# A third gate/up column pair by seven products, and first weight sums of the output products by accumulating transfers

## The chip, the core and the metric

The kernel runs on one core of a Trainium2 chip. TensorE (PE in the profile) multiplies, ScalarE (ACT) and VectorE (DVE) prepare weights and finish results, GpSimd (POOL) takes a few roots and issues accumulating DMAs, and SyncE (SP) issues the other DMAs. The metric is the device time of one execution in microseconds (us); of several runs the median counts.

## The reference

Two layers of a decoder trunk work on 256 tokens with 1024 channels. In each layer a retention mixer and a state-space (SSD) mixer feed a gated sum, and a SwiGLU feed-forward network (FFN) with 2816 hidden columns follows. What the change touches is in these lines:

```python
o_ret = yr @ ret_out                      # 2048 -> 1024
o_ssd = ys @ ssd_out                      # 2048 -> 1024
merged = sigmoid(gate_ret) * o_ret + sigmoid(gate_ssd) * o_ssd
h = h + merged @ w_o
...
gu = rmsnorm(h, norm_ffn_w) @ w_gate_up   # 1024 -> 2 * 2816
gate, up = split(gu, [2816])
h = h + (silu(gate) * up) @ w_down        # 2816 -> 1024
```

## The kernel before

**Precision.** Every float32 operand is split in two float32r parts, a high one and the rest. A product is three matmuls: high by high, high by low, low by high (`mm3`, L542). For a weight piece of 128x1024 the split is one ACT instruction (`wh`, L506) and one DVE subtraction (`wl`, L527). Seven pairs of `wh` and `wl` buffers are there (`HB`, L200): a piece can be split at most seven pieces ahead of TensorE.

**Three ways to compute a pair of FFN columns.** The hidden columns are cut into five pairs of 512 gate and 512 up columns, and a half pair (number 5, `NPAIR`). `FFN` (L1142) lists how each is computed, in the order of the jobs.
- `plain`: eight weight pieces, 96 matmuls of 512 columns, and the result of each token tile is transposed (`up_post`, L1939) since the down product needs it with channels on partitions.
- `fm` (`fm_job`, L970): four jobs, also eight pieces. The weights stand still and the tokens move, so the result comes out transposed already. A job has two blocks, each with eight matmuls of 512 columns and eight of 256.
- `seven` (`sevens`, L359, and `wino_job`, L911): the 2x2 block product of two token tiles by two halves of the 1024 channels by gate and up columns, with seven block products in place of eight: 84 matmuls of 512 columns. It needs sums of weight blocks: t1 = 11 + 12, t2 = t1 + 22, t3 = 12 + 22, t4 = t2 + 21. Each of the seven (11, t1, t2, 22, t3, 21, t4) is two pieces, so 14 pieces are split. The tokens' sums are made once per layer (`seven_sums`, L675), on DVE and ACT, and the results of the blocks are put together on DVE. Its result is transposed as in `plain`.

`GF` (L32) names the pairs whose weights are laid out for `fm`.

**Sums of weights.** A sum is either a DVE addition (L230 in the profile) or, where `added` names it, a DMA that POOL issues and that adds weights from DRAM to the buffer in place (L416). Such a DMA can only be issued when both splits of what stood in the buffer have been made, and the next split waits until it has landed.

**Output products.** `out_wino` (L1057) does a part of each of `ret_out`, `ssd_out` and `w_down` by seven products and the other rows of the weights plainly, one 128x1024 piece at a time, with four blocks (two token tiles t0, t1 by two column halves) of three matmuls each. An order such as `AMID` (L294, for `w_down`) says how the seven products and the plain pieces (`"*"`) follow each other. The plain pieces that the order doesn't name come last, and block by block: all of them for t0 and the first half of the columns, then t0 and the second half, then t1 twice. So the residual sum, the norm and the transposition for t0 can begin while TensorE still works for t1. `w_down` has 14 plain pieces; `AMID` names nine of them, and five are left for the end.

**Order of the work.** The kernel plans itself while it is built: every step is put on its engine's instruction list when a model of the engines, with priorities by job number, says that it is due (`Flow`). On the chip each engine then works through its list strictly in that order, and an instruction that waits holds up all behind it. Raw weight pieces land in four `raw` buffers; the seven products also use two buffers called `raws` (block 11) and two called `cc` (block 12), or `dec` in the retention product.

Of the kernel before, what the change touches and what calls it, by code (L numbers as in the profile page):

```python
# [27 lines left out]
NPAIR = FF // 512  # L28
C_Q, C_K, C_V, C_G, C_Z, C_X, C_DT, C_GR, C_GS = 0, 1024, 2048, 4096, 6144, 8192, 11264, 11296, 12320
NB = 24  # L30

GF = (1, 3, NPAIR)  # L32


DW = 1
# [157 lines left out]
def trunk_kernel(  # L193
# [66 lines left out]
    ccS, new_cc = pooled(tp, (P, D), F32, "cc", 2)  # L260
# [30 lines left out]
    ALONE = ("11", "t1", "t2", "22", "t3", "21", "t4")  # L291


    AMID = ("*", "*", "*", "*", "11", "*", "t1", "*", "t2", "22", "*", "t3", "*", "21", "*", "t4")  # L294

    SMID = ("*", "*", "11", "*", "t1", "*", "t2", "22", "*", "t3", "21", "t4")

# [759 lines left out]
    def out_wino(op, nk, at, tag, order, post, add, ops):  # L1057
# [74 lines left out]
        for t in range(NT):  # L1132
# [7 lines left out]


    FFN = [[("plain", 0)],  # L1142
           [("fm", 1)],
           [("seven", (2,), ("t3", "t4"))],
           [("fm", 3)],
           [("seven", (4,), ("t3", "t4"))],
           [("fm", NPAIR)]]
    DIRECT = ()
    DOWN_APART = ()

# [14 lines left out]
    def add_layer_jobs(l):  # L1165
        def srcs_of(kind, *at):
            if kind == "gr":
                return tm_srcs(w_gr[l, at[0]])
            if kind in FM:
                return fm_srcs(w_fm[l, FM[kind] + at[0] + (at[0] + at[1] if len(at) > 1 else 0)])  # L1170
            if kind in ("ret", "ssd", "wo"):
                return out_srcs({"ret": ret_out, "ssd": ssd_out, "wo": w_o}[kind][l])
            return tm_srcs(w_tm[l, TM[kind] + at[0]], kper=1 if l == 0 and (kind, *at) == ("v", 0) else 2)

        def adds_of(kind, *at, order=MIXED):
            if kind == "seven":
                c = TM[at[0]] + at[1]
                return [sevens(w_tm[l, c], w_tm[l, c + 1], added=at[2], order=order, slots=None)]
            return [plain((srcs_of(kind, *at), APARTS.get((kind, *at), ())))]

        for m in MIXERS[l]:
            if m == ("ret",):
                group(sevens(w_rw[l, 0], w_rw[l, 1], added=("t3", "t4"), order=RMID, first=RET_FIRST),
                      plain((out_srcs(ret_out[l])[8:], RET_APART)))
            elif m == ("ssd",):
                group(sevens(w_sw[l, 0], w_sw[l, 1], added=("t3", "t4"), order=SMID, slots=(ccS, new_cc)),
                      plain((out_srcs(ssd_out[l])[8:], ())))
            elif isinstance(m, tuple):
                for add in adds_of(*m, order=ALONE):
                    group(add)  # L1190
            else:
                group(*(chain(*(a for j in stream for a in adds_of(*j))) for stream in m))
        for members in FFN:
            adds = []
            for kind, *at in members:
                if kind == "seven":
                    adds.append(chain(*(sevens(w_gate_up[l, 0, c], w_gate_up[l, 1, c], added=at[1], order=ALONE if len(members) == 1 else ASIDE,
                                               slots=(ccS, new_cc)) for c in at[0])))
                elif kind == "fm":
                    adds.append(plain(*((srcs, APART) for c in at for srcs in gf_srcs(l, c))))  # L1200
                else:
                    adds.append(plain(*((srcs, APART) for c in at for srcs in gate_up_srcs(l, c))))
            group(*adds)
        lone = [s for k, s in enumerate(out_srcs(w_down[l])) if k // 4 not in (DW, DW + 1)]
        group(sevens(w_dw[l, 0], w_dw[l, 1], added=("t3", "t4"), order=AMID, slots=(ccS, new_cc)),
              plain((lone, DOWN_APART)))

    def params(l, done):
# [1011 lines left out]
```

## Time and profile before

| | |
|---|---|
| Median of 3 runs | 1253.82 us (1253.73 to 1256.33) |
| The profiled execution's own time | 1254.82 us |
| Its span, first to last instruction | 1253.0 us |
| Instructions in it | 17610 |
| Moved by DMA | 266.27 MB, mean 213 GB/s |
| FFN of the first layer on TensorE | about 450 to 629 us |
| FFN of the second layer | about 1069 us to the end |

A page of the profile gives busy times, the chain of work that ended last, and groups of instructions by line. The trace behind it can be asked for single instructions in order of time ("the timeline"), for busy times in stretches ("the windows"), and for the instructions of one line with their shortest, median and longest duration. Matmuls overlap in their pipeline: a row shows 0.39 us for a matmul of 512 columns, while the next one starts after about 0.23 us. So costs on TensorE are read from start to start. The same holds on DVE, where instructions overlap a little.

### The profile page before, as it was taken

How to read it: one execution, taken by the hardware profiler on the slowest of the kernel's cores; microseconds unless marked ns; L12 is line 12 of the kernel's file. 1: busy time of each engine (PE TensorE's matmuls, PEld its weight loads, DVE VectorE, ACT ScalarE, POOL GpSimd, SP SyncE). 2: the span in 40 equal slices, each digit the busy share in tenths (PEclk: the TensorE clock that was granted, in tenths of full speed). 3: DMA queues.
4: the chain of work that ended last, by engine and by line, in shares of the span. 5: the costliest groups of instructions: out<-in, count | busy, mean ns of one | idle time of the engine just before them, and what ended most of it. 6: DMA issues, size and time to landing. Idle time of an engine off the chain costs nothing.

```text
span 1253.0 us, 17610 instructions
## 1 busy us (share of the span) xinstructions
PE 1241.8 (99%) x6286; PEld 1051.5 (84%) x6286; DVE 1108.0 (88%) x1516; ACT 885.2 (71%) x1307; POOL 67.2 (5%) x92
## 2 busy tenths in 40 slices
PE   9999999999999999999999999999999999999997
PEld 7889888888888888888888898888888888888886
DVE  6997888789999978999888888888899998899995
ACT  6866778877776566776586676878877674776753
POOL 0000000000002001001000000000010110010000
PEclk9999999999999999999999999999999999999999
DMA  8758565456768657877777475555667676678872
GB/s 289 253 145 285 182 187 166 152 190 185 258 232 225 233 187 226 296 210 215 256 249 235 112 259 167 188 168 165 217 179 241 240 231 218 216 212 252 290 205 85
DMA packets 76343, 266.27 MB, mean 213 GB/s; under 512 B 8768, under 2 KB 9024, under 8 KB 76256
## 3 DMA queue, kind: packets, MB, share of 16 engines
q1 hardware_dynamic: 68416, 237.25, 55.8%
q0 software_dynamic: 7552, 27.38, 11.7%
q8 instruction: 49, 0.80, 0.3%
q10 hardware_dynamic: 288, 0.52, 0.1%
q14 instruction: 38, 0.31, 0.1%
HBM read 262.96 MB, written 2.16 MB: 212 GB/s over the span
## 4 chain that ended last, share of the span: by engine, by line
PE 91%; ACT 4%; DVE 2%; issue 1%; DMA 1%; SPq 0%; POOL 0%; POOLq 0%; ACTq 0%; DVEq 0%
PE acc L543 19%; PE acc L545 19%; PE acc L544 19%; PE acc L988 14%; PE acc L989 8%; PE tr L640 2%; PE yps L1699 2%; PE acc L991 2%; ACT wh L506 1%; DVE wl L527 1%; ACT seg L1667 1%; PE acc L1421 1%; PE tr L1592 1%; DMA raw<-in_w_gr_dram 1%; DMA raw<-in_w_tm_dram 1%
## 5 line engine op out<-in xcount | busy, mean ns | idle before, releaser
L527 DVE TENSOR_TENSOR wl<-raw,wh 128x1024 fp32r<-128x1024 f32 (+2 forms) x388 | 458.4, 1195 | 52.7 <-ACT wh L506 48.7
L506 ACT ACTIVATE wh<-raw 128x1024 fp32r<-128x1024 f32 (+2 forms) x388 | 397.2, 1035 | 148.2 <-PE acc L545 37.1
L988 PE MATMUL acc<-xT,wh 128*128 128x512 f32 x840 | 303.8, 399 | 0.3 <-DVE cc L230 0.3
L989 PE MATMUL acc<-xT,wl 128*128 128x256 f32 x960 | 252.2, 281 | 0.0
L543 PE MATMUL acc<-wh,xT 128*128 128x512 f32 (+1 forms) x568 | 220.1, 387 | 0.0
L545 PE MATMUL acc<-wh,xT 128*128 128x512 f32 (+1 forms) x568 | 216.1, 380 | 0.0
L544 PE MATMUL acc<-wl,xT 128*128 128x512 f32 (+1 forms) x568 | 216.1, 380 | 0.0
L989 PEld LDWEIGHTS acc<-xT,wl 128*128 128x128 f32 x960 | 181.2, 189 | 10.1
L988 PEld LDWEIGHTS acc<-xT,wh 128*128 128x128 f32 x840 | 158.0, 188 | 32.9 <-PE acc L991 0.6
L544 PEld LDWEIGHTS acc<-wl,xT 128*128 128x128 f32 x568 | 106.7, 188 | 20.2 <-issue 1.0
L543 PEld LDWEIGHTS acc<-wh,xT 128*128 128x128 f32 x568 | 106.7, 188 | 19.5 <-issue 1.4
L545 PEld LDWEIGHTS acc<-wh,xT 128*128 128x128 f32 x568 | 106.6, 188 | 19.5
L506 ACT ACTIVATE wh<-raws 128x1024 fp32r<-128x1024 f32 x80 | 83.5, 1057 | 32.0 <-DVE raws L230 12.9
L527 DVE TENSOR_TENSOR wl<-raws,wh 128x1024 fp32r<-128x1024 f32 x80 | 96.3, 1220 | 7.9 <-ACT wh L506 7.5
L543 PE MATMUL acc<-wh,A 128*128 128x512 f32 x224 | 89.9, 402 | 0.3
L545 PE MATMUL acc<-wh,A 128*128 128x512 f32 x224 | 87.5, 390 | 0.0
L544 PE MATMUL acc<-wl,A 128*128 128x512 f32 x224 | 87.3, 390 | 0.0
L233 DVE SCALAR_TENSOR_TENSOR cc<-cc,cv 128x255 f32<-128x255 f32 (+1 forms) x144 | 67.1, 478 | 2.5 <-ACT cc L223 1.6
L223 ACT ACT_TABLE_LOAD x43 | 55.2, 1283 | 6.1 <-DVE cc L233 5.5
L543 PE MATMUL acc<-wh,C 128*128 128x512 f32 (+1 forms) x152 | 59.3, 390 | 0.0
L544 PE MATMUL acc<-wl,C 128*128 128x512 f32 (+1 forms) x152 | 58.4, 384 | 0.9 <-DVE wl L527 0.9
L545 PE MATMUL acc<-wh,C 128*128 128x512 f32 (+1 forms) x152 | 58.2, 383 | 0.0
(197 smaller groups left out, 1999.7 us busy)
## 6 DMA issues: line engine op xcount, KB each, us to landing
raw<-in_w_tm_dram SPq DMA_DIRECT2D x104, 512.0 KB, 4.2
raw<-in_w_fm_dram SPq DMA_DIRECT2D x80, 512.0 KB, 4.2
raw<-in_w_gf_dram SPq DMA_DIRECT2D x40, 512.0 KB, 4.6
raw<-in_w_gate_up_dram SPq DMA_DIRECT2D x32, 512.0 KB, 6.3
raw<-in_w_down_dram SPq DMA_DIRECT2D x28, 512.0 KB, 4.7
raw<-in_w_gr_dram SPq DMA_DIRECT2D x24, 352.0 KB, 3.9
seg<-acs SPq DMA_DIRECT2D x16, 512.0 KB, 5.1
raw<-in_ret_out_dram SPq DMA_DIRECT2D x16, 512.0 KB, 4.2
```

The costliest lines, as they stand in the source:

```text
L223: return Op("act", cost, lambda: nc.scalar.activation(out=out, in_=in_, func=func, **kw), pr, TABLES.get(func))
L233: return Op("dve", 1.04 * n + 130, lambda: nc.vector.scalar_tensor_tensor(out=out, in0=in0, scalar=scalar, in1=in1, op0=op0, op1=op1), pr)
L506: nc.scalar.activation(out=wh[:, :m], in_=raw[:, :m], func=AF.Copy)
L527: nc.vector.tensor_tensor(out=wl[:, :m], in0=raw[:, :m], in1=wh[:, :m].bitcast(F32), op=ALU.subtract)
L543: nc.tensor.matmul(ps, lhsT=lh, rhs=rh, start=first, stop=False, **kw)
L544: nc.tensor.matmul(ps, lhsT=lh, rhs=rl, start=False, stop=False, **kw)
L545: nc.tensor.matmul(ps, lhsT=ll, rhs=rh, start=False, stop=last, **kw)
L640: nc.tensor.transpose(out=ps[:, j * P : (j + 1) * P], in_=src[:, j * P : (j + 1) * P], identity=ident)
L988: nc.tensor.matmul(a, lhsT=wh[:, k % 4, fsl], rhs=x[:, k % 4, :, :], start=k == 0, stop=False)
L989: nc.tensor.matmul(a[:, :SEQ], lhsT=wl[:, k % 4, fsl], rhs=xh[:, k % 4, :], start=False, stop=False)
L991: nc.tensor.matmul(a, lhsT=wh[:, k % 4, fsl], rhs=x[:, k % 4, :, :], start=False, stop=True)
L1699: nc.tensor.matmul(ps[:, i * HD : (i + 1) * HD], lhsT=sg[:, i, :], rhs=xdt[:, i * HD : (i + 1) * HD], start=True, stop=True)
```

## The change

Three things are edited.
- `FFN` and `GF`: before, the pairs ran as plain 0, fm 1, seven 2, fm 3, seven 4, fm half pair 5. Now they run as plain 0, seven 1, fm 2, seven 3, fm half pair 5, seven 4. So per layer one `fm` pair becomes a `seven` pair, and a seven pair now follows the plain pair at once, one follows the half pair, and one stands directly ahead of the down product.
- `added=("t1", "t3", "t4")` for the sevens of `ret_out`, `ssd_out` and `w_down`: the first sum, t1, is made by an accumulating DMA and no longer on DVE. As block 12 is then needed in a buffer for t3 alone, its load is placed later (`need`, L375). The sevens of the FFN pairs keep t1 on DVE.
- `AMID`: eight plain pieces ahead of the first seven-product block instead of four, eleven named instead of nine. Three are left for the end instead of five.

```diff
-GF = (1, 3, NPAIR)
+GF = (2, NPAIR)
...
-    AMID = ("*", "*", "*", "*", "11", "*", "t1", "*", "t2", "22", "*", "t3", "*", "21", "*", "t4")
+    AMID = ('*', '*', '*', '*', '*', '*', '*', '*', '11', '*', 't1', '*', 't2', '22', '*', 't3', '21', 't4')
...
     FFN = [[("plain", 0)],
-           [("fm", 1)],
-           [("seven", (2,), ("t3", "t4"))],
-           [("fm", 3)],
-           [("seven", (4,), ("t3", "t4"))],
-           [("fm", NPAIR)]]
+           [("seven", (1,), ("t3", "t4"))],
+           [("fm", 2)],
+           [("seven", (3,), ("t3", "t4"))],
+           [("fm", NPAIR)],
+           [("seven", (4,), ("t3", "t4"))]]
...
-                group(sevens(w_rw[l, 0], w_rw[l, 1], added=("t3", "t4"), order=RMID, first=RET_FIRST),
+                group(sevens(w_rw[l, 0], w_rw[l, 1], added=("t1", "t3", "t4"), order=RMID, first=RET_FIRST),
...
-                group(sevens(w_sw[l, 0], w_sw[l, 1], added=("t3", "t4"), order=SMID, slots=(ccS, new_cc)),
+                group(sevens(w_sw[l, 0], w_sw[l, 1], added=("t1", "t3", "t4"), order=SMID, slots=(ccS, new_cc)),
...
-        group(sevens(w_dw[l, 0], w_dw[l, 1], added=("t3", "t4"), order=AMID, slots=(ccS, new_cc)),
+        group(sevens(w_dw[l, 0], w_dw[l, 1], added=("t1", "t3", "t4"), order=AMID, slots=(ccS, new_cc)),
```

What that does to the engines' lists shows at three places.

The first is on DVE in the first layer, right behind the plain pair, while the tokens' sums (`plain`, `D`) are made; `wl` is the low part of a weight piece, `raws` and `raw` the blocks 11 and 22 or pieces of an fm pair, `sil` and `A` the plain pair's result. Before, these twelve rows stood there:

```order
L230 TENSOR_TENSOR plain_4449<-plain_4449,plain_4537 128x512
L527 TENSOR_TENSOR wl_4610<-raw_4524,wh_4594 128x1024
L230 TENSOR_TENSOR D_4609<-plain_4449,D_4608 128x4x128
L230 TENSOR_TENSOR plain_4531<-plain_4425,plain_4531 128x512
L527 TENSOR_TENSOR wl_4628<-raw_4576,wh_4617 128x1024
L527 TENSOR_TENSOR wl_4639<-raw_4584,wh_4630 128x1024
L230 TENSOR_TENSOR D_4609<-plain_4531,D_4608 128x4x128
L527 TENSOR_TENSOR wl_4661<-raw_4603,wh_4646 128x1024
L230 TENSOR_TENSOR sil_4502<-acc_4503,sil_4502 128x512
L230 TENSOR_TENSOR sil_4586<-acc_4587,sil_4586 128x512
L527 TENSOR_TENSOR wl_4686<-raw_4622,wh_4670 128x1024
L230 TENSOR_TENSOR sil_4694<-acc_4667,sil_4694 128x256
```

Now twelve rows of the same stretch, up to the `wl` of t2's second piece (`wl_4720`), are these:

```order
L230 TENSOR_TENSOR raws_4480<-raws_4480,cc_4494 128x1024
L230 TENSOR_TENSOR D_4613<-plain_4539,D_4612 128x4x128
L230 TENSOR_TENSOR raws_4475<-raws_4475,raw_4499 128x1024
L230 TENSOR_TENSOR sil_4510<-acc_4511,sil_4510 128x512
L230 TENSOR_TENSOR sil_4592<-acc_4593,sil_4592 128x512
L527 TENSOR_TENSOR wl_4668<-raws_4480,wh_4645 128x1024
L527 TENSOR_TENSOR wl_4673<-raws_4475,wh_4657 128x1024
L230 TENSOR_TENSOR raws_4480<-raws_4480,raw_4507 128x1024
L230 TENSOR_TENSOR A_4663<-tr_4676,A_4662 128x4x128
L230 TENSOR_TENSOR A_4663<-tr_4682,A_4662 128x4x128
L527 TENSOR_TENSOR wl_4710<-raw_4507,wh_4699 128x1024
L527 TENSOR_TENSOR wl_4720<-raws_4480,wh_4708 128x1024
```

The additions of weight blocks (`raws<-raws`) now stand among the tokens' sums, and t2's second low part stands behind both of its sums. The second layer has the same rows.

The second place is DVE's list between the end of the first layer's down product and the second layer. `O` is the residual, two buffers for t0 and t1; `ms` belongs to the norm, `sil` is the normed input, `xT` its transposed low part, `wl` are weights of the second layer. Before:

```order
L230 TENSOR_TENSOR O_3863<-O_3863,acc_5624 128x512
L238 TENSOR_SCALAR ms_6037<-ss_6036,ms_6018 128x1
L233 SCALAR_TENSOR_TENSOR sil_6048<-O_3863,rstd_6043,wb_5620 128x512
L233 SCALAR_TENSOR_TENSOR sil_6049<-O_3863,rstd_6043,wb_5620 128x512
L230 TENSOR_TENSOR O_3866<-O_3866,acc_5629 128x512
L230 TENSOR_TENSOR xT_6055<-tr_6057,xT_6055 128x4x128
```

Now:

```order
L230 TENSOR_TENSOR O_3860<-O_3860,acc_5575 128x512
L527 TENSOR_TENSOR wl_6030<-raw_5977,wh_6017 128x1024
L238 TENSOR_SCALAR ms_6016<-ss_6015 128x1
L238 TENSOR_SCALAR ms_6029<-ss_6028,ms_6016 128x1
L230 TENSOR_TENSOR O_3864<-O_3864,acc_5583 128x512
L527 TENSOR_TENSOR wl_6060<-raw_5989,wh_6037 128x1024
L233 SCALAR_TENSOR_TENSOR sil_6055<-O_3860,rstd_6046,wb_5570 128x512
L233 SCALAR_TENSOR_TENSOR sil_6056<-O_3860,rstd_6046,wb_5570 128x512
L230 TENSOR_TENSOR O_3864<-O_3864,acc_5590 128x512
L238 TENSOR_SCALAR ms_6059<-ss_6058 128x1
L527 TENSOR_TENSOR wl_6094<-raw_5995,wh_6049 128x1024
L230 TENSOR_TENSOR xT_6074<-tr_6077,xT_6074 128x4x128
```

Three weight splits and both residual sums of t1 now stand between t0's last residual sum and the first `xT`. On TensorE the transposition of t0 (`tr_6057` before, `tr_6077` now) stood ahead of the last block of the down product before; now it stands behind it.

The third place is POOL's list in the SSD output product of the first layer; `rz` is a root of the norm there, `raws` holds block 11 and then t1, t2, t4, and `cc` holds block 12 and then t3. The rows with + are new, the one with - goes:

```order
 L668 DMA wb<-in_ssd_norm_w_dram 128x1024
+L416 DMA raws<-in_w_sw_dram 128x1024
+L243 TENSOR_TENSOR rz<-ms,mhalf 128x1 x2
+L416 DMA raws<-in_w_sw_dram 128x1024
 L243 TENSOR_TENSOR rz<-ms,mhalf 128x1 x2
 L416 DMA cc<-in_w_sw_dram 128x1024 x2
-L243 TENSOR_TENSOR rz<-ms,mhalf 128x1 x2
 L668 DMA wb<-in_norm_ffn_w_dram 128x1024
 L416 DMA raws<-in_w_sw_dram 128x1024 x2
```

The two new DMAs make t1. The pairs of roots that stood around the `cc` transfers now stand behind one or both of them.

## The prediction

> **What bounds the kernel now.** I read the page's busy times first, then the chain that ended last, then the windows of the first layer's FFN, where most of the change lies.
>
> ```profile
> PE 1241.8 (99%) x6286; PEld 1051.5 (84%) x6286; DVE 1108.0 (88%) x1516; ACT 885.2 (71%) x1307; POOL 67.2 (5%) x92
> ...
> PE 91%; ACT 4%; DVE 2%; issue 1%; DMA 1%; SPq 0%; POOL 0%; POOLq 0%; ACTq 0%; DVEq 0%
> ```
>
> TensorE is busy for 99% of the span and carries 91% of the chain. DVE is next with 88%. So time is won where TensorE gets less to do, as long as DVE, which prepares its weights, doesn't fall behind. The windows below go from one job's first matmul to the next one's: plain 0, fm 1, seven 2, fm 3, seven 4, the half fm, the down product.
>
> ```profile
> core 0: us, PE busy (x) PEld busy (x) DVE busy (x) ACT busy (x) POOL busy (x), PEclk, DMA share, GB/s
> 450.45:473.32 22.87, 22.87 (x106) 19.03 (x105) 20.71 (x26) 17.28 (x24) 0.55 (x1) 1.00 0.66 220
> 473.32:496.76 23.44, 23.44 (x138) 20.46 (x137) 20.01 (x25) 13.61 (x20) 2.61 (x3) 1.00 0.80 238
> 496.76:515.80 19.04, 19.04 (x85) 15.77 (x84) 19.03 (x21) 15.73 (x19) 0.88 (x1) 1.00 0.78 215
> 515.80:539.20 23.40, 23.40 (x137) 20.48 (x136) 21.19 (x26) 15.35 (x23) 2.60 (x3) 1.00 0.88 274
> 539.20:558.24 19.04, 19.04 (x85) 15.77 (x84) 19.02 (x21) 15.73 (x19) 0.87 (x1) 1.00 0.79 215
> 558.24:570.37 12.13, 12.13 (x74) 10.68 (x72) 9.29 (x12) 8.72 (x13) 0.00 (x0) 1.00 0.96 372
> 570.37:628.80 58.43, 58.27 (x261) 48.02 (x260) 51.45 (x62) 34.04 (x44) 4.58 (x6) 1.00 0.71 211
> ```
>
> Three things stand there. TensorE has no gap in the pairs, at full clock (1.00). While it does a seven pair, DVE is full (19.03 of 19.04 us). DVE's total over the seven windows is 160.70 us (the sum of their third column), TensorE's 178.35.
>
> ```profile
> L543 PEld LDWEIGHTS acc<-wh,xT 128*128 128x128 f32 x568 | 106.7, 188 | 19.5 <-issue 1.4
> 496.75 0.40 PE L543 MATMUL acc<-wh,xT 128*128 128x512 f32 x1
> 513.08 0.39 PE L543 MATMUL acc<-wh,xT 128*128 128x512 f32 x1
> ```
>
> Between the last two rows lie 72 matmuls of seven 2, so one starts 0.227 us after the other, and each has a weight load of 0.188 us, 83% of that. The Trainium skill, "Perfetto Trace Analysis", section "Identifying the Most-Contended Engine", says that matmul busy time tells little about how full TensorE is and that weight-load busy time is the better measure. By it the page's 84% would leave 16% to win without less work; the 83% inside a row without gaps says that 84% is full here, and the sum below is unchanged.
>
> **TensorE's gain.** Per layer an fm pair goes and a seven pair comes.
>
> ```profile
> 473.32 0.39 PE L988 MATMUL acc<-xT,wh 128*128 128x512 f32 x1
> ...
> 475.90 0.40 PE L991 MATMUL acc<-xT,wh 128*128 128x512 f32 x1
> 476.13 1.03 PE L640 MATMUL tr<-cst,sil 128*128 128x128 f32 x8
> ...
> 477.25 0.28 PE L989 MATMUL acc<-xT,wl 128*128 128x256 f32 x1
> ```
>
> The first block of fm 1 runs from 473.32 to 0.23 behind 475.90: 2.81 us, and a pair has eight. The eight transpositions that plain and seven results need, set into the next job, cost 1.35 us from 475.90 to 477.25 less the two matmuls of 0.23 around them: 0.88. The windows of fm 1 and fm 3 less this are 22.56 and 22.52, so an fm pair takes 22.54. A seven pair takes 19.04 (its window). So a pair saves 22.54 - 19.04 - 0.88 = 2.62 us, and the two layers **5.24 us**.
>
> **DVE's price.**
>
> ```profile
> 481.40 1.23 DVE L527 TENSOR_TENSOR wl<-raws,wh 128x1024 fp32r<-128x1024 f32 x1 [0.20 <-ACT wh L506]
> 482.66 1.22 DVE L230 TENSOR_TENSOR raws<-raws,cc 128x1024 f32<-128x1024 f32 x1
> ...
> 507.01 2.35 DVE L527 TENSOR_TENSOR wl<-raws,wh 128x1024 fp32r<-128x1024 f32 x2
> ...
> 608.37 4.63 DVE L527 TENSOR_TENSOR wl<-raw,wh 128x1024 fp32r<-128x1024 f32 x4
> ```
>
> Four splits in a row take 4.63, so a further one costs (4.63 - 1.22)/3 = 1.14 us; an addition takes the same 1.22 by itself. A seven pair has 14 splits and 4 additions of 1.14 (20.5) and eight combinations of about 0.6: 25.3 us. An fm pair has eight splits (9.1) and its combinations, some 5.1: 14.2. DVE gets 11.1 us more per layer, and the down product's t1 by DMA takes two additions (2.3) away. That makes 169.5 us in the FFN against 175.7 on TensorE: 96%. It fits on the whole; the question is where it doesn't in places.
>
> Where a seven pair follows a full fm pair, as seven 3 does, nothing differs from before: the first low part of seven 2 is made at 481.40, more than 14 us ahead of 496.75, and its last pair ends at 509.36, some 5 us ahead of its use near 514.7. Seven 4 now follows a half fm. DVE's work for both is 7.1 + 25.3 = 32.4 us, TensorE's 12.13 + 19.04 = 31.17; with those 5 us at the start some 3.9 us remain at the end. I cost it at nothing; its cover is that lead.
>
> **Seven 1 behind the plain pair** has no such start.
>
> ```profile
> 460.01 0.69 DVE L230 TENSOR_TENSOR plain<-plain 128x512 f32<-128x512 f32 x1 [0.67 <-ACT plain L223]
> 461.40 0.69 DVE L230 TENSOR_TENSOR D<-plain,D 128x512 fp32r<-128x512 f32 x1 [0.70 <-ACT D L223]
> ```
>
> From this `plain` row to the second low part of t2 (`wl_4720`) the new list has 24 rows: eight splits and four additions at 1.14, and twelve of about 0.61: 21.0 us. The wait ahead of `D` leaves 0.78 us empty (461.40 less 460.01 and 0.61), and I allow 0.2 for one wait for `wh` as in the row at 481.40. So that low part is there at 460.01 + 21.0 + 1.0 = 482.0, and is seen 0.1 later. TensorE begins seven 1 at 473.32, does two pieces of 11 (six matmuls, 1.36 us each), the transpositions (0.88), two of t1, the first of t2 and one matmul: 481.2. It waits **0.9 us**. Behind it DVE gives a piece each 1.14 us and TensorE takes 1.36, so it isn't repeated. Queued behind the waiting matmul are only matmuls of the same pair. Bounds: 0, if the small rows take the 0.33 us that they have elsewhere, and 3, if three more of the ACT waits (0.67 and 0.70 above) aren't filled. I take 0.9, from the rows nearest to it; twice: **+1.8**.
>
> **The layer's end.** With three pieces left for the end, not five, TensorE has less to do between t0's last block and the next layer.
>
> ```profile
> 620.69 0.39 PE L543 MATMUL acc<-wh,C 128*128 128x512 f32 x1
> ...
> 623.87 0.39 PE L545 MATMUL acc<-wh,Y 128*128 128x512 f32 x1
> 624.41 0.66 PE L640 MATMUL tr<-cst,sil 128*128 128x128 f32 x4 [0.16 <-DVE sil L233]
> ...
> 633.33 0.39 PE L545 MATMUL acc<-wh,xT 128*128 128x512 f32 x1
> 634.04 0.63 PE L640 MATMUL tr<-cst,sil 128*128 128x128 f32 x4 [0.32 <-DVE sil L233]
> ```
>
> t1's first block starts at 620.69 (call it zero). Before, two gaps stood here: 624.41 less 623.87 and 0.23 is 0.31, and likewise 0.48 at 634.04: 0.79 us. Now t1's two blocks are 2 x 3 x 3 x 0.227 = 4.08 us, and the transpositions stand behind both.
>
> ```profile
> 621.24 0.68 DVE L230 TENSOR_TENSOR O<-O,acc 128x512 f32<-128x512 f32 x1
> 622.71 0.21 DVE L238 TENSOR_SCALAR ms<-ss,ms 128x1 f32<-128x1 f32 x1 [0.79 <-ACT sil L223]
> 623.60 1.42 DVE L233 SCALAR_TENSOR_TENSOR sil<-O,rstd,wb 128x512 f32<-128x512 f32 x2 [0.68 <-POOL rstd L243]
> ...
> 625.73 0.69 DVE L230 TENSOR_TENSOR xT<-tr,xT 128x512 fp32r<-128x512 f32 x1
> ```
>
> DVE's new list from t0's residual sum, which starts at 0.55: the sum 0.60, a split 1.14, two small rows 0.36, t1's sum 0.60, a split 1.14, the first norm row 0.66: done at 5.1, where TensorE was free at 4.08. Then the second norm row 0.66, t1's other sum 0.60, a small row 0.15, a third split 1.14 and `xT` 0.60: 8.3. TensorE would want `xT` behind both transpositions and its first high-by-high matmuls, at 4.08 + 0.88 + 0.45 = 5.4. It waits 2.9 us in all, in place of 0.79: **+2.1**. Behind it on its list stand only the next layer's first products. Bounds: 0, if the third split finds its place in a gap, and 3.5, if each split is held by `wh` once (0.20). At the kernel's end no splits are in the list, and I cost it at 0 to 0.3.
>
> **The added transfers.**
>
> ```profile
> q1 hardware_dynamic: 68416, 237.25, 55.8%
> q0 software_dynamic: 7552, 27.38, 11.7%
> ...
> cc<-in_w_dw_dram POOLq DMA_DIRECT2D x4, 512.0 KB, 6.0
> raws<-in_w_sw_dram POOLq DMA_DIRECT2D x4, 512.0 KB, 7.1
> L416 POOL DMA_DIRECT2D raws<-in_w_gate_up_dram x8: 854/860/882, 494.8 to 1159.1; - x8
> ```
>
> Twenty are added on POOL: twelve make t1, eight t3 and t4 of the new pairs. q0 moved 27.38 MB, some 52 pieces of 512 KB, in 11.7% of the span: 2.8 us of all DMA engines each. Six per FFN add 17 us to a mean share of about 0.76, to 0.86; the half fm window shows 0.96 without a gap on TensorE. For t1 in the SSD product:
>
> ```profile
> 374.43 1.22 DVE L527 TENSOR_TENSOR wl<-raws,wh 128x1024 fp32r<-128x1024 f32 x1
> ...
> 395.98 0.39 PE L543 MATMUL acc<-wh,A 128*128 128x512 f32 x1
> ```
>
> The first low part of 11 is done at 375.6, t1 is wanted at 396.0. Issue 0.9, landing 7.1, `wh` 1.1 and `wl` 1.2 make 10.3, so 10 us are left, of which the piece that shares the queue takes some. In the down product the same path (9.2 with 6.0 to land) lies beside up to seven split pieces of 1.36 to 2.72 us, about 13. The roots that move behind one issue come 0.86 later, beside matmuls. I take 0; from below, up to 0.5 could be gained by the 1.14 us of each addition, from above 1 in all.
>
> A rule of the Trainium skill speaks against these transfers: "SBUF — State Buffer", section "SBUF: two separate sides", has GpSimd locked out of writing descriptors while DVE runs an operation in a two-port mode. It would hold them up just where DVE is full. The row of L416 speaks against it: 854 to 882 ns per issue, all beside a DVE that is busy in the windows above.
>
> **Sum.** -5.24 + 1.8 + 2.1 = -1.3 us. The profiled execution took 1254.82 us (span 1253.0), which gives 1253.5; it was 1.0 above the median of the runs, so **1252.5**.
>
> **Rivals.** *DVE keeps up everywhere.* The small rows overlap, and the third split at the layer's end finds a gap: both waits go, -5.2, 1248.6. For it: TensorE never waited in the FFN before. Against it: the lists' strict order. 0.22.
>
> *Seven 1 waits longer.* The `plain` and `D` rows wait for ACT again and again, since one big row now stands between them where two stood. With the 2.1 at the layer's end the kernel is slower than before once each wait is over (5.24 - 2.1)/2 = 1.6 us. With three more ACT waits of 0.7 it is 3.0: -5.24 + 6.0 + 2.1 = +2.9, 1256.7. For it: both rows above wait. Against it: only the first ones did; later ones found other rows ahead. 0.15.
>
> *The transfers are held up while DVE is full*, as a mechanism of this kernel: t3 or t4 would miss its place once landing takes over about 11 us, and where it lasts for a whole full stretch (19 us), each new seven waits some 8 us: 1252.5 + 16 = 1268. Against it: the issues of 0.86 us and landings of 6 to 7. The skill's rule named above is this one. 0.03.
>
> **How the numbers follow.** The forecast has 0.60. About 0.2% (2.5 us) is what a measurement of this kernel can tell from no change: 1251.3 to 1256.3. Faster: the first rival and 0.08 of the forecast with waits near their lower bounds, 0.30. Slower: half of the second rival, the third, and 0.02 of the forecast, 0.13. Same: 0.57. The range takes in the first rival and most of the second: 1248.5 to 1256.6.
>
> **What would show it.** The matmul rows fall by 72, and the windows of seven pairs stay at 19.04. A gap of about 0.9 us on TensorE's L544 row, ended by `wl`, about 8 us into seven 1, in both layers; none in seven 3 and 4. At the second layer's start gaps of about 1.0 ahead of the transpositions and 1.9 ahead of L545 or L543 with `xT`. Landings on POOL's queue of 5 to 9 us. The prediction is wrong if gaps stand in seven 4 (the lead was too small), if t1's L506 in an output product waits for a DMA with TensorE idle, or if seven 1's gap repeats piece after piece.

## The result and the profile after

The changed kernel takes **1272.55 us** (median of four runs, 1271.4 to 1274.28) against 1254.67 before: ratio 1.0147, 95% interval 1.0135 to 1.0159. It is 18 us slower, and 20 us above the forecast of 1252.5, whose range ended at 1256.6.

The page of the profile after, its busy times, the chain that ended last, and POOL's DMA queue:

```profile
PE 1245.3 (98%) x6214; PEld 1042.3 (82%) x6214; DVE 1113.8 (88%) x1516; ACT 888.2 (70%) x1309; POOL 89.8 (7%) x112
...
q0 software_dynamic: 10432, 37.86, 16.1%
...
PE 49%; DVE 21%; DMA 13%; issue 8%; ACT 6%; POOL 1%; SPq 0%; POOLq 0%; DVEq 0%; ACTq 0%
```

TensorE has its 72 matmuls less (6286 to 6214), and yet the chain of work no longer runs through it: 49% instead of 91%. DVE has 21% and DMA 13%. The averages hide this, since TensorE is still busy for 98% and DVE for the same 88%. The windows of the first layer's FFN, from plain 0 to the next layer (plain, seven 1, fm 2, seven 3, half fm, seven 4, down product):

```profile
core 0: us, PE busy (x) PEld busy (x) DVE busy (x) ACT busy (x) POOL busy (x), PEclk, DMA share, GB/s
452.52:475.17 22.65, 22.65 (x106) 18.84 (x104) 20.96 (x26) 15.29 (x22) 2.13 (x3) 1.00 0.77 256
475.17:495.95 20.78, 20.28 (x94) 16.51 (x92) 19.42 (x22) 15.27 (x19) 1.91 (x3) 1.00 0.74 177
495.95:519.72 23.77, 23.70 (x138) 20.42 (x137) 22.23 (x28) 14.77 (x23) 1.73 (x2) 1.00 0.90 290
519.72:539.16 19.44, 19.35 (x85) 15.69 (x84) 19.13 (x22) 16.57 (x20) 1.73 (x2) 1.00 0.87 244
539.16:552.34 13.18, 12.36 (x74) 10.62 (x73) 13.18 (x17) 7.20 (x12) 1.73 (x2) 1.00 0.83 279
552.34:571.74 19.40, 19.33 (x85) 15.69 (x84) 19.12 (x21) 15.67 (x19) 2.28 (x3) 1.00 0.85 235
571.74:636.13 64.39, 61.20 (x270) 48.27 (x268) 54.06 (x65) 37.84 (x49) 5.72 (x7) 1.00 0.83 242
```

Each window is compared with what the job takes in the windows of before: plain 22.65 (its first matmul is at 450.67, 0.22 behind the start of its window of 22.87), seven 19.04, fm 22.54, half fm 11.24, the down product 58.43 and 56.90, and 0.88 for each pair that is transposed within. The waits are the differences:

| stretch | as before | layer 1 | waits | layer 2 | waits |
|---|---|---|---|---|---|
| plain and seven 1 | 42.57 | 43.43 | 0.86 | 44.63 | 2.06 |
| fm 2 | 23.42 | 23.77 | 0.35 | 23.88 | 0.46 |
| seven 3 | 19.04 | 19.44 | 0.40 | 19.07 | 0.03 |
| half fm | 12.12 | 13.18 | 1.06 | 12.63 | 0.51 |
| seven 4 | 19.04 | 19.40 | 0.36 | 19.42 | 0.38 |
| down product | 59.31, 57.78 | 64.39 | 5.08 | 60.84 | 3.06 |

(The down product of layer 2 is taken to its last matmul.) That is 8.1 us of waits in the first FFN and 6.5 in the second. The mixers have 6.7 more: from the first SSD output matmul to the FFN 68.1 and 68.3 us instead of 66.5 twice, and from the second layer's first matmul to its SSD output product 377.1 instead of 373.7 (with the last wait of the layer's end, below). In all 21.3, less the 5.24 gained: 16.1 of the 16.3 us by which the last matmul starts later.

TensorE's timeline in the first FFN shows what ended the waits (in brackets the idle time and its releaser):

```profile
483.75 0.50 PE L544 MATMUL acc<-wl,D 128*128 128x512 f32 x1 [0.50 <-DVE wl L527]
...
543.65 0.66 PE L640 MATMUL tr<-cst,sil 128*128 128x128 f32 x4 [0.82 <-DVE sil L230]
...
621.72 0.50 PE L543 MATMUL acc<-wh,Y 128*128 128x512 f32 x1 [1.77 <-ACT sx L223]
...
634.81 1.29 PE L640 MATMUL tr<-cst,sil 128*128 128x128 f32 x8 [0.71 <-DVE sil L233]
637.78 0.50 PE L545 MATMUL acc<-wh,xT 128*128 128x512 f32 x1 [0.92 <-DVE xT L230]
```

The first is the wait in seven 1, in its place (8.6 us in) and of its size. The last two are the layer's end, in their places but smaller: from start to start they are 0.86 and 1.09 us, 1.9 together, where 2.9 were forecast. Those between were not forecast: a transposition that waits for the results of seven 3, and t4's first matmul in the down product, which waits until ACT has taken earlier results out of an accumulator. What held ACT and DVE up there shows on DVE's own timeline in the down product, on POOL's and on ACT's:

```profile
588.63 1.23 DVE L527 TENSOR_TENSOR wl<-raws,wh 128x1024 fp32r<-128x1024 f32 x1
...
591.51 0.69 DVE L230 TENSOR_TENSOR D<-plain,D 128x512 fp32r<-128x512 f32 x1
596.83 1.23 DVE L527 TENSOR_TENSOR wl<-raws,wh 128x1024 fp32r<-128x1024 f32 x1 [4.63 <-ACT wh L506]
...
600.65 1.23 DVE L527 TENSOR_TENSOR wl<-raws,wh 128x1024 fp32r<-128x1024 f32 x1 [1.34 <-ACT wh L506]
...
617.40 1.23 DVE L527 TENSOR_TENSOR wl<-raws,wh 128x1024 fp32r<-128x1024 f32 x1
621.22 1.22 DVE L527 TENSOR_TENSOR wl<-raws,wh 128x1024 fp32r<-128x1024 f32 x1 [2.59 <-ACT wh L506]
```

```profile
588.48 0.86 POOL L416 DMA_DIRECT2D raws<-in_w_dw_dram  x1 [29.48 <-DVE wl L527]
590.46 0.87 POOL L416 DMA_DIRECT2D raws<-in_w_dw_dram  x1 [1.12 <-DVE plain L230]
...
608.04 0.86 POOL L416 DMA_DIRECT2D raws<-in_w_dw_dram  x1 [1.55 <-DVE wl L527]
```

```profile
620.13 1.06 ACT L506 ACTIVATE wh<-raws 128x1024 fp32r<-128x1024 f32 x1 [2.76 <-DMA raws<-in_w_dw_dram]
621.09 0.58 ACT L223 ACTIVATE sx<-acc 128x512 f32<-128x512 f32 x1
```

At 588.5 and 590.5 the transfers for t1 are issued, as soon as 11 is split. DVE then does what it has, and stands still for 4.63 and 1.34 us: the next row of its list is the low part of t1, and the transfers must land first. At 608.04 the second transfer for t4 is issued; it lands at 620, 12 us later by the chain of waits, and DVE waits 2.59 us for it. ACT waits for it too (620.13), and the `sx` row that empties the accumulator for t4's first matmul stands behind that wait on its list. Two windows and the view of DMA issues (the last number is us to landing) show the DMA engines meanwhile:

```profile
590.00:600.00 10.00, 10.00 (x46) 8.28 (x45) 4.65 (x5) 2.14 (x3) 0.87 (x1) 1.00 0.97 252
...
610.00:621.00 11.00, 9.96 (x44) 7.89 (x43) 7.58 (x8) 5.01 (x5) 0.00 (x0) 1.00 1.04 304
```

```profile
raws<-in_w_dw_dram POOLq DMA_DIRECT2D x8, 512.0 KB, 9.5
```

The DMA engines are full (0.97 and 1.04) just then, while DVE is idle for half of the first stretch. They are not the whole of it: the four transfers of t3 and t4 are issued within 6.7 us (601.32, 602.58, 605.64, 608.04) and land in the same order at 606.7, 612.4, 616.2 and 620.1, after 5.4, 9.8, 10.6 and 12.0 us. So they seem to stand one behind another on POOL's queue as well. The change took 2.3 us of additions off DVE here, and DVE stood still for 6.0 us in front of t1 and 2.6 in front of t4.

### The profile page after: what moved, and what is told of

The parts are those of the page before. It is cut to its first block, busy times and chain, and to the rows that moved or that the text cites. A ratio compares the mean times of both kernels' runs of the same rounds, so it can differ in the third digit from the quotient of the medians.

```text
span 1270.1 us, 17507 instructions
## 1 busy us (share of the span) xinstructions
PE 1245.3 (98%) x6214; PEld 1042.3 (82%) x6214; DVE 1113.8 (88%) x1516; ACT 888.2 (70%) x1309; POOL 89.8 (7%) x112
## 3 DMA queue, kind: packets, MB, share of 16 engines
q0 software_dynamic: 10432, 37.86, 16.1%
## 4 chain that ended last, share of the span: by engine, by line
PE 49%; DVE 21%; DMA 13%; issue 8%; ACT 6%; POOL 1%; SPq 0%; POOLq 0%; DVEq 0%; ACTq 0%
DVE wl L527 11%; PE acc L988 10%; PE acc L543 8%; PE acc L544 8%; PE acc L545 8%; PE acc L989 6%; ACT wh L506 3%; DMA raws<-in_w_dw_dram 3%; DMA raws<-in_w_gate_up_dram 3%; DMA raws<-in_w_sw_dram 2%; DVE sx L230 2%; DVE plain L230 2%; PE yps L1699 2%; PE acc L991 2%; PE tr L640 1%
## 5 line engine op out<-in xcount | busy, mean ns | idle before, releaser
L527 DVE TENSOR_TENSOR wl<-raw,wh 128x1024 fp32r<-128x1024 f32 (+2 forms) x380 | 449.4, 1195 | 46.5 <-ACT wh L506 44.8
L506 ACT ACTIVATE wh<-raw 128x1024 fp32r<-128x1024 f32 (+2 forms) x380 | 386.4, 1034 | 125.7 <-DMA raw<-in_w_tm_dram 28.2
L988 PE MATMUL acc<-xT,wh 128*128 128x512 f32 x728 | 263.4, 399 | 0.3 <-DVE cc L230 0.3
L543 PE MATMUL acc<-wh,xT 128*128 128x512 f32 (+1 forms) x592 | 229.5, 388 | 1.0 <-ACT sx L223 0.9
L545 PE MATMUL acc<-wh,xT 128*128 128x512 f32 (+1 forms) x592 | 225.6, 381 | 0.9 <-DVE xT L230 0.9
L544 PE MATMUL acc<-wl,xT 128*128 128x512 f32 (+1 forms) x592 | 225.5, 381 | 0.0
L989 PE MATMUL acc<-xT,wl 128*128 128x256 f32 x832 | 219.5, 282 | 0.3 <-DVE wl L527 0.2
L989 PEld LDWEIGHTS acc<-xT,wl 128*128 128x128 f32 x832 | 157.0, 189 | 9.5 <-DVE wl L527 0.9
L506 ACT ACTIVATE wh<-raws 128x1024 fp32r<-128x1024 f32 x96 | 101.2, 1059 | 84.5 <-DVE raws L230 32.6
L988 PEld LDWEIGHTS acc<-xT,wh 128*128 128x128 f32 x728 | 136.9, 188 | 28.4 <-PE acc L991 0.6
L527 DVE TENSOR_TENSOR wl<-raws,wh 128x1024 fp32r<-128x1024 f32 x96 | 116.7, 1222 | 25.6 <-ACT wh L506 25.1
```

Source lines behind the costliest of these rows:

```text
L506: nc.scalar.activation(out=wh[:, :m], in_=raw[:, :m], func=AF.Copy)
L527: nc.vector.tensor_tensor(out=wl[:, :m], in0=raw[:, :m], in1=wh[:, :m].bitcast(F32), op=ALU.subtract)
L543: nc.tensor.matmul(ps, lhsT=lh, rhs=rh, start=first, stop=False, **kw)
L544: nc.tensor.matmul(ps, lhsT=lh, rhs=rl, start=False, stop=False, **kw)
L545: nc.tensor.matmul(ps, lhsT=ll, rhs=rh, start=False, stop=last, **kw)
L988: nc.tensor.matmul(a, lhsT=wh[:, k % 4, fsl], rhs=x[:, k % 4, :, :], start=k == 0, stop=False)
```

## The experiments

Theory A: the transfers for t1 are the cost. Theory B: the new order of the down product is. Theory C: the new places of the FFN pairs are. The first four kernels do one part alone, or leave one out. All are compared with the kernel before on the same chip; its median was 1254.13, 1253.86 and 1254.41 us in the three sets, so that the medians below can be set side by side to about half a microsecond.

**t1 by transfers alone**, the three FFN and order edits undone:

```diff
-added=("t3", "t4"), order=RMID   (and SMID, AMID)
+added=("t1", "t3", "t4"), order=RMID   (and SMID, AMID)
```

> The kernel before with t1 of ret_out, ssd_out and w_down made by accumulating transfers, and nothing else. Theory A (the transfers: block 11's sums t1, t2, t4 stand on one buffer one behind the other, so a landing of 6 to 12 us for t1 delays t2 and t4, and TensorE waits where ACT and DVE wait for them): most of the 22 us of new waits come from this, +6 us in the mixers (retention and SSD output products) and +3 to +5 in the down products: 1262 to 1266 us. Theory B (the order of the down product with three pieces at the end is the cost): the mixers still lose their 6 us, the down products nothing: about 1260. Theory C (the new places of the FFN pairs are the cost, since DVE's lead is gone ahead of the down product): at most +2, 1254 to 1256.

Measured: 1258.46 us, ratio 1.0036 (1.0026 to 1.0047). Nine runs lie between 1254.69 and 1260.51, before's between 1252.66 and 1256.87. Less than theory A wanted, more than C, and nearest to B's 1260. The cost differs from run to run. The profile is of the fastest of the nine; its down products take 58.12 and 56.90 us, no more than before. Where the 4.3 us of the median lie is not shown by it.

**The new order of the down product alone** (`AMID`):

> The kernel before with the new order of the down product alone (eight plain pieces first, three left for the end). Theory A: only the layer's end waits, as predicted +2.1: about 1256. Theory B: the whole 8 us of the down products of both layers comes with it: about 1262. Theory C: about 1254 to 1256.

Measured: 1256.33 us, ratio 1.0015 (1.0005 to 1.0024): +2.2. Theory B falls. The number is the 2.1 that was predicted for the layer's end, but the profile puts only part of it there. From the down product's first matmul to the next layer's first matmul of L988 the two kernels take 79.24 (568.79 to 648.03) and 78.39 us before (570.37 to 648.76), 0.85 more. Another 0.8 stands at the kernel's end. The last matmuls of this kernel and of the one before are

```profile
1245.22 0.39 PE L545 MATMUL acc<-wh,Y 128*128 128x512 f32 x1
1245.59 0.39 PE L545 MATMUL acc<-wh,Y 128*128 128x512 f32 x1
```

and the spans end at 1253.4 and 1253.0, so 8.2 us follow instead of 7.4. In the changed kernel it is 8.2 too (1261.93 to 1270.1).

**The new FFN pairs alone** (`FFN` and `GF`):

> The kernel before with the new list of FFN pairs alone (three seven pairs at places 1, 3 and 4). TensorE's gain of 5.24 us, less the waits measured inside the FFN pairs of the changed kernel (2.9 us in seven 1, 3.5 us in the jobs behind it, both layers together). Theories A and B: -5.2 + 6.4 = +1.2, about 1255. Theory C: the down products wait too, +5 to +8 more: 1260 to 1263.

Measured: 1263.93 us, ratio 1.0075 (1.0058 to 1.0091), just above theory C's range. Its down products take 63.4 us instead of 59.3, and 62.05 instead of 57.8. TensorE's timeline in the first of them:

```profile
587.31 0.50 PE L544 MATMUL acc<-wl,D 128*128 128x512 f32 x1 [0.81 <-DVE wl L527]
591.92 0.50 PE L544 MATMUL acc<-wl,A 128*128 128x512 f32 x1 [1.22 <-DVE wl L527]
```

The waits stand at t1 and at the plain piece behind it, and they are for DVE's low parts: with four plain pieces ahead of 11, and seven 4 ahead of those, DVE comes to the sums without a lead.

**New pairs and new order, t1 on DVE:**

> The changed kernel without its transfers for t1: the new FFN pairs and the new order of the down product, t1 by DVE as before. Theory A: the mixers' 6 us and most of the down products' go: 1257 to 1260 (-5.2 + 6.4 + 2.1 = +3.3). Theory B: only the mixers' 6 us go: about 1266. Theory C: as B or higher, since DVE also has t1's additions back.

Measured: 1259.51 us, ratio 1.0044 (1.0027 to 1.0061), as A. The order that costs 2.2 us with the old pairs saves 4.4 with the new ones (1263.93 to 1259.51). The down products are back at 60.5 and 58.2, so its eight plain pieces seem to give DVE time behind seven 4. And the transfers are the largest part: 1259.51 to 1272.55.

**Where the transfers cost: the mixers alone, the down product alone** (on the changed kernel, t1 back on DVE in the others):

> The changed kernel with t1 by transfers in ret_out and ssd_out alone; in the down product DVE adds it as before. Theory A (transfers): without any for t1 it was 1259.5, with all 1272.55. In the changed kernel's trace the down products are 6.5 us longer than without them (3.9 in the first layer, 2.6 in the second), the mixers 5.6. If the down product's transfers and the mixers' add up: 1259.5 + 5 = 1264 to 1266. If the transfers only hurt where the new FFN pairs leave DVE no lead (theory A2): 1260 to 1262.

> The changed kernel with t1 by transfers in the down product alone. Theory A: the down products' 6.5 us stay: 1265 to 1267. Theory A2: most of the 13 us between 1259.5 and 1272.55 stay, 1269 or more. If it is the mixers' alone: 1260.

Measured: 1263.53 us, ratio 1.0072 (1.0054 to 1.009), and 1268.67 us, ratio 1.0121 (1.0102 to 1.014). Against 1259.51 the mixers' transfers cost 4.0 us and the down product's 9.2. Together that is 13.2, and the whole difference is 13.0: the two add up. The mixers lie between the ranges of theories A2 and A, the down product above A's and just below A2's 1269.

**Does the down product's transfer cost only without a lead?** The kernel before with the new order and t1 of the down product by transfers (the two new lines):

```diff
+    AMID = ('*', '*', '*', '*', '*', '*', '*', '*', '11', '*', 't1', '*', 't2', '22', '*', 't3', '21', 't4')
+        group(sevens(w_dw[l, 0], w_dw[l, 1], added=("t1", "t3", "t4"), order=AMID, slots=(ccS, new_cc)),
```

> The kernel before (old FFN pairs) with the new order of the down product and t1 of the down product alone by transfers. With the new FFN pairs these transfers cost 9.2 us. Theory F (they cost only where DVE comes to block 11 without a lead: the transfer can't be issued before 11's splits, and DVE and ACT stand still until it has landed): with the half pair ahead of the down product the lead is there, and it takes as long as with the new order alone, 1255 to 1257. Theory G (the new order with eight plain pieces first puts the sums of the seven products too close together, so that landings of 9 to 12 us don't fit, whatever stands ahead): 1262 to 1266.

Measured: 1257.6 us, ratio 1.0026 (1.0016 to 1.0035), 0.6 above theory F's range and far from G. It is 3.2 us above the kernel before, where the order alone was 2.2: the same transfers in the same order cost about 1 us here, against 9.2. Its first transfer on POOL, and DVE's row that waits for it:

```profile
579.66 0.86 POOL L416 DMA_DIRECT2D raws<-in_w_dw_dram  x1 [38.33 <-DVE plain L230]
```

```profile
586.13 1.23 DVE L527 TENSOR_TENSOR wl<-raws,wh 128x1024 fp32r<-128x1024 f32 x1 [0.40 <-ACT wh L506]
```

It is issued 10.2 us into the down product (which starts at 569.5), not 16.7 us into it (588.48 less 571.74), and DVE waits 0.40 us for it instead of 4.63. It also lands faster, 5.3 us after its issue instead of 7.2. But a long landing alone is not the cost: t4's transfers take 9.8 and 12.3 us here (10.6 and 12.0 in the changed kernel).

**Is it DVE's work that the FFN pairs lack?** The additions for t1 and t2 in the seven pairs are left out:

```diff
+            elif "-" + q in added:
+                yield raw
             else:
                 w = yield raw
                 yield tt(D, pr, x, x, w, ALU.add)
...
+           [("seven", (1,), ("t3", "t4", "-t1", "-t2"))],   (3 and 4 too)
```

> The new FFN pairs and the new order of the down product, t1 by DVE in the output products (1259.51 so far), and the additions for t1 and t2 left out in the FFN's seven pairs, so that their products use block 11 instead. That takes 4 x 1.14 = 4.6 us of DVE's 25.3 per seven pair away, and leaves TensorE's work the same. Theory D (the pairs' waits come from DVE, which has no lead where seven pairs stand behind plain, half and each other's short rests): of the 10.4 us of waits in the two FFNs some 8 go, 1250 to 1253, below the kernel before. Theory E (the waits come from PSUM buffers and results whatever DVE has to do, or from transfers): 1258 to 1260.

Measured: 1251.32 us, ratio 0.9977 (0.9967 to 0.9986), as theory D. Its windows in the first FFN (plain with seven 1, fm 2, seven 3, half fm, seven 4):

```profile
450.02:492.60 42.58, 42.58 (x197) 35.45 (x196) 40.59 (x47) 33.27 (x43) 4.04 (x5) 1.00 0.82 247
492.60:515.98 23.38, 23.38 (x137) 20.48 (x136) 16.79 (x23) 15.31 (x23) 2.60 (x3) 1.00 0.85 274
515.98:535.03 19.05, 19.05 (x85) 15.77 (x84) 19.02 (x21) 16.93 (x20) 0.86 (x1) 1.00 0.90 272
535.03:547.13 12.10, 12.10 (x73) 10.67 (x72) 9.27 (x13) 7.70 (x12) 2.60 (x3) 1.00 1.00 269
547.13:566.19 19.06, 19.06 (x85) 15.77 (x84) 19.03 (x21) 15.78 (x19) 1.42 (x2) 1.00 0.83 242
```

All stand at their durations without waits, those of the accumulators and results too. With 4.6 of 25.3 us less per seven pair DVE has time again in fm 2 (16.79 of 23.38 us busy, 22.23 of 23.77 in the changed kernel). A full DMA (1.00 in the half pair) costs nothing there. The edit takes out the wait of a split for its sum together with the sum's time, so it doesn't tell these two apart.

**Another order of the pairs**, with the seven pairs 3 and 4 side by side:

```diff
-GF = (2, NPAIR)
+GF = (1, NPAIR)
+    FFN = [[("plain", 0)], [("fm", 1)], [("seven", (2,), ("t3", "t4"))],
+           [("fm", NPAIR)], [("seven", (3,), ("t3", "t4"))], [("seven", (4,), ("t3", "t4"))]]
```

> The same three seven pairs per layer in another order: plain 0, fm 1, seven 2, half fm, seven 3, seven 4, with the new order of the down product and t1 by DVE. Theory D, by running leads: seven 2 starts with some 14 us and waits nowhere, seven 3 starts with 5 + 5 = 10 and ends with 3, seven 4 has 6.3 us too little and waits 3 to 4 us, and the down product starts without a lead and waits 1 to 2 more: 4 to 6 us per layer, about as much as the 5.2 per layer of the new order: 1258 to 1262. Theory E: as long as the changed order, 1259.5, with waits of the same kinds in every seven pair, seven 2 too.

Measured: 1269.15 us, ratio 1.0119 (1.0104 to 1.0134). The place was right, the size not: seven 2, the half pair and fm 1 wait nowhere (19.05, 12.13 and 23.43 us), the waits of the FFN's pairs stand in the two neighbours, but there they are 7.2 us in the first layer and 7.6 in the second instead of 3 to 4. (Of the 7.2 some 1.5 are TensorE's clock: at 554.00 to 557.75 the granted clock is 0.55, with 3.38 us busy, and 3.38 x 0.45 is 1.5, an estimate. The second layer has no such stretch.) SyncE's timeline and TensorE's in seven 4:

```profile
540.27 1.46 SPq L488 DMA_DIRECT2D raws<-in_w_gate_up_dram  x2
```

```profile
553.43 0.50 PE L544 MATMUL acc<-wl,D 128*128 128x512 f32 x1 [1.22 <-DVE wl L527]
```

Block 11 of seven 4 is loaded at 540.27 only, when seven 3's t4 has been split (DVE's row at 539.03): the pairs share the two `raws` buffers. So a lead that is there can't be used for the next pair's block 11.

**t1 by transfers in the FFN's pairs**, on the kernel with new pairs and order:

```diff
+           [("seven", (1,), ("t1", "t3", "t4"))],   (3 and 4 too)
```

> The new FFN pairs and the new order of the down product, t1 by DVE in the output products but by transfers in the FFN's seven pairs. DVE has 2 x 1.14 us less per seven pair, as it had 4 x 1.14 less where leaving out t1 and t2 took 1259.5 to 1251.3. If only DVE's work counts: half of that, about 1255. Theory F: DVE has no lead at a seven pair's block 11 either, so a landing of 5 to 9 us stands in its list between 11 and t1 and costs more than it saves: 1262 or more.

Measured: 1304.12 us, ratio 1.0394 (1.0378 to 1.0409). It takes 2.3 us of work per pair off DVE, and the time rises by 44.6 us. DVE's timeline at seven 4:

```profile
566.27 1.23 DVE L527 TENSOR_TENSOR wl<-raws,wh 128x1024 fp32r<-128x1024 f32 x1 [7.00 <-ACT wh L506]
```

Seven us of DVE go in front of one row, as theory F has it. The size is not the landing's alone. In this pair t1's second transfer is issued behind both of t3's (557.86, 559.35 and then 560.15) and lands 12.3 us later. And TensorE's clock falls behind the waits:

```profile
568.00:578.00 10.00, 5.87 (x14) 3.78 (x13) 6.74 (x7) 4.54 (x5) 0.87 (x1) 0.50 0.22 37
```

The seventh number is the granted clock, 0.50; in the FFN windows of the changed kernel it is 1.00. Busy time at the lower clock, times the share that is missing, gives an estimate of what this costs: about 10 us over the four such stretches of the run.

**Block 12 loaded early again**, on the changed kernel:

```diff
-                need = [c for c in need if c not in added or c not in ("t1", "t2")]
+                need = [c for c in need if c not in added or c != "t2"]
```

> The changed kernel with block 12 of the output products loaded as early as before (at t1's place in the order instead of t3's), t1 still by transfers. Theory F: the load's place matters little, 1270 to 1274. Theory H (the later loads of 12 push t3's transfers against t4's, and the DMA engines are full at 610 to 621 us): t4 lands earlier, and the 1.8 and 1.0 us in the down products that end with its evictions go: 1267 to 1270.

Measured: 1285.86 us, ratio 1.0245 (1.0228 to 1.0262). Both expectations fell, by 12 us and more. POOL's timeline and DVE's in the first down product:

```profile
591.95 0.86 POOL L416 DMA_DIRECT2D cc<-in_w_dw_dram  x1 [28.90 <-DVE plain L230]
592.99 0.87 POOL L416 DMA_DIRECT2D raws<-in_w_dw_dram  x1 [0.19 <-issue]
```

```profile
604.51 1.23 DVE L527 TENSOR_TENSOR wl<-raws,wh 128x1024 fp32r<-128x1024 f32 x1 [7.79 <-ACT wh L506]
```

With 12 there early, t3's transfer (`cc`) goes ahead of t1's (`raws`) on POOL, and the four are issued within 4 us: DVE waits 7.79 us for t1 instead of 4.63. So the later load in the change was no mistake, and the order on POOL's queue counts: t1's first transfer takes 10.3 us to land, not 7.2. Part of the rise is TensorE's clock again. Two windows, ahead of the fall and in it:

```profile
603.00:609.50 6.50, 3.22 (x12) 1.77 (x10) 2.96 (x3) 2.58 (x4) 0.00 (x0) 1.00 0.73 148
609.75:616.75 7.00, 6.54 (x16) 4.78 (x17) 7.00 (x7) 6.22 (x7) 0.86 (x1) 0.53 0.33 92
```

The second costs 6.54 x 0.47 = 3.1 us by the same estimate, and with two other stretches of the run it is about 6.5 of the 13.3 us above the changed kernel.

**t1 of the FFN's pairs on POOL**, as an instruction, on the kernel with new pairs and order:

```diff
-                yield tt(D, pr, x, x, w, ALU.add)
+                yield (pool if "p" + q in added else tt)(D, pr, x, x, w, ALU.add)
...
+           [("seven", (1,), ("pt1", "t3", "t4"))],   (3 and 4 too)
```

> The new FFN pairs and the new order of the down product, t1 by DVE in the output products, and t1 of the FFN's seven pairs added by a POOL instruction (128x1024) instead of DVE's. Theory D: DVE's relief of 2.3 us per seven pair is worth half of what leaving t1 and t2 out was, about 1255; a POOL addition of 2 to 3 us instead of 1.2 delays t1 by 1 to 2 us and eats part of it: 1255 to 1258. If POOL and DVE hinder each other on the buffers: 1260 or more.

Measured: 1269.01 us, ratio 1.0115 (1.01 to 1.013), 9.5 more than with DVE's additions. POOL's timeline and DVE's in seven 1:

```profile
464.30 2.77 POOL L243 TENSOR_TENSOR raws<-raws,cc 128x1024 f32<-128x1024 f32 x1 [10.50 <-DVE wl L527]
```

```profile
464.74 3.41 DVE L527 TENSOR_TENSOR wl<-raws,wh 128x1024 fp32r<-128x1024 f32 x1
```

A split that takes 1.22 us elsewhere takes 3.41 beside POOL's addition: it ends 1.08 us after POOL does. Beside each of the twelve additions one DVE row is stretched in this way. DVE is not relieved but blocked. None of the kernels that compute everything beats the one before.

## Why the prediction was wrong, step by step

**TensorE's gain of 5.24 us was right.** Where the pairs wait for nothing (the kernel without the sums), the five windows above make 116.2 us against 119.70 before (450.67 to 570.37, the start of the down product), with one set of transpositions (0.88) gone into the down product: 2.65 per layer, predicted 2.62. That kernel's time is 2.5 us below before's, and the forecast for such a kernel would be -5.24 + 2.1 = -3.1.

**The layer's end, +2.1, came out as a number, and by luck:** 2.2 us with the order alone, but in its profile 0.85 stand there. In the changed kernel the two waits make 1.9 us against 0.79 before, 1.2 more and not 2.1. The kernel's end, costed at 0 to 0.3, takes 0.8. So the waits were in their places, the first was too large and the second too small. Some 0.5 of the 2.2 us are not placed.

**Seven 1, 0.9 us per layer, was right in mechanism and too small in one layer:** 0.86 and 2.06. The second layer has a further wait, for an accumulator that ACT empties late.

**"Where a seven pair follows a full fm pair, as seven 3 does, nothing differs from before" was wrong.** The fm pair is the same, but what stands ahead of it isn't: fm 1 followed plain, fm 2 follows seven 1, which leaves no lead. DVE's row of the first low part of seven 3:

```profile
509.61 2.53 DVE L527 TENSOR_TENSOR wl<-raws,wh 128x1024 fp32r<-128x1024 f32 x2 [0.40 <-ACT wh L506]
```

Its first low part is there at about 510.8, 9.1 us ahead of its use at 519.95, where seven 2 had 14.4 (482.6 to 497.0). The 5 us at the start of the half pair that the working took over are some 3.1, read in the same way (534.9 to 538.0). I followed the lead through single pairs and not through the list. And I counted only weights: fm 2 waits for a low part, but the half pair, where the transposition waits, and seven 4, whose wait ends behind an `sx` row of ACT, wait for results that DVE or ACT fetched late. From fm 2 to seven 4 these waits cost 3.6 us in both layers together, 2.3 of them in the half pair and seven 4. All were forecast at nothing.

**The down product behind seven 4 got no term at all.** The 3.9 us that seven 4 was to leave were not carried on into it: with the new pairs alone it waits 4.1 and 4.3 us. The change's third edit, which I counted as a loss of 2.1, repairs most of it. Its sign depends on the pairs ahead.

**The added transfers, costed at nothing, were the largest error: 13.0 of the 20 us by which the forecast missed.** (The other 6.7 are the new pairs with the new order: 1259.51 is 5.4 above the kernel before, where -1.3 was forecast.) Two steps failed there. In the down product I took "up to seven split pieces of 1.36 to 2.72 us, about 13" as the cover of a path of 9.2 us. Behind seven 4 that cover isn't there: the low part of the first piece of 11 is done at 588.1, 6.5 us ahead of its use at 594.7. With the half pair ahead the same transfers cost about 1 us, not 9.2. And I asked only whether TensorE needs t1 in time, not what DVE does until it lands. It follows its list, so it stands still (4.63 and 1.34 us), and what stands behind on the list is late afterwards: t2, t4, the results. In the mixers the 10 us left for t1 were there, and t4 was late instead: DVE's row of its second low part in the first SSD product, and the transposition behind it on TensorE.

```profile
411.29 1.22 DVE L527 TENSOR_TENSOR wl<-raws,wh 128x1024 fp32r<-128x1024 f32 x1 [1.66 <-ACT wh L506]
```

```profile
425.61 0.63 PE L640 MATMUL tr<-cst,D 128*128 128x128 f32 x4 [1.31 <-DVE D L230]
```

Why such transfers with the old pairs cost 4.3 us in the median, and next to nothing in the fastest of nine runs, is not settled: only that fastest run has a profile.

**The rivals.** Seven 1 waiting longer (2.06 in one layer) was a small part. The one that came nearest, transfers that miss their place while DVE is full, had 0.03 of the chance and gave 1268. Its outcome was right, its mechanism as I put it was not: the issues in the down product still take 0.86 us each (rows at 588.48 to 608.04), and DVE stands idle for 4.63 us while t1's transfers are on their way, so it isn't a busy DVE that holds them. The landings are long while the DMA engines are full with other loads and four transfers are issued close together on POOL's queue; how much each adds is not shown. A few issues elsewhere do take longer, up to 1.49 us at 295.49 in the retention product, the third of three in a row. What holds these is not shown.

**The range** was too narrow since "no wait" was taken for seven 3, seven 4, the down product and the transfers there at once, and the cover of all four was the same DVE lead. They failed together.

## What to carry to other kernels

Two engines at 99% and 88% left no room here for a trade of 2.6 us of the one against 11 us of the other: carry the second engine's lead through the whole list of jobs, and count its results as well as its inputs. In these runs a DMA in place of an engine's instruction was cheap only where the engine had other rows to do until it landed (about 1 us with the old pairs); without them the landing time stood in its place on the engine's list (9.2 us). An edit that reads as a loss by itself can be the repair of another one, so such edits are priced together.

## What the runs showed of the hardware that was not expected

An addition of 128x1024 on POOL took 2.77 us (2.39 to 3.40 over the twelve), and a DVE subtraction on SBUF beside it 3.41 instead of 1.22 us. The Trainium skill, "SBUF — State Buffer", section "SBUF: two separate sides", says that POOL and a DVE instruction with two SBUF inputs exclude each other on a shared port for a whole instruction; the row agrees. An accumulating transfer of 512 KB landed 5.2 to 12.0 us after its issue in the changed kernel, with a median of 9.5 in the down product where the DMA share was 0.97 to 1.04; before, the same view had 6.7 there.

TensorE's granted clock fell to about half behind long waits, in three kernels only. With block 12 early, TensorE was busy for 3.22 of 6.50 us, and the next 7 us show a clock of 0.53; with the pairs 3 and 4 side by side, it was busy for 4.19 of 6.00 us (548 to 554), and the next 3.75 show 0.55; with t1 of the pairs by transfers there were four such stretches. In the changed kernel, with single waits of up to 1.77 us, there is none before the last matmul.
